# A hybrid decoder block: a pair of heads' projections between the first and second recurrent tile, w2's copies in even parts

## The chip, the cores and the metric

The kernel runs on one core of a Trainium2 chip. The metric is the device time of one execution in microseconds (us), lower is better. The core has TensorE (PE, matmuls; PEld is its weight load), VectorE (DVE), ScalarE (ACT), GpSimd (POOL) and the sync engine (SP, which here only issues transfers), and 16 DMA engines that all queues share.

## The reference, cut to what matters

```python
D_MODEL, SEQ, N_ATTN_HEADS, HEAD_DIM, LRU_WIDTH, CONV_WIDTH, D_FF = 1024, 2048, 8, 64, 512, 4, 4096
DILATED_PATTERNS = ((128, 1), (512, 4), (2048, 16))

def hybrid_mixer(h, w_in, conv_w, conv_b, w_r, b_r, w_i, b_i, lam, w_out):
    z = h @ w_in
    q, k, v, xr, gr = jnp.split(z, [512, 1024, 1536, 2048], axis=-1)
    attn = dilated_attention(q, k, v)          # 8 heads, three windows, joined by their denominators
    xr = causal_depthwise_conv(xr, conv_w, conv_b)
    rec = rg_lru(xr, w_r, b_r, w_i, b_i, lam) * jax.nn.gelu(gr)
    return jnp.concatenate([attn, rec], axis=-1) @ w_out

def rg_lru(x, w_r, b_r, w_i, b_i, lam):
    r, i = sigmoid(x @ w_r + b_r), sigmoid(x @ w_i + b_i)      # block by block
    log_a = -LRU_C * r * jax.nn.softplus(-lam)
    a, u = jnp.exp(log_a), jnp.sqrt(-jnp.expm1(2.0 * log_a)) * (i * x)
    return scan(h[t] = a[t] * h[t-1] + u[t])

def reference(x, ...):
    h = rms_norm(x, mix_norm_pre)
    x = x + rms_norm(hybrid_mixer(h, ...), mix_norm_post)
    h = rms_norm(x, mlp_norm_pre)
    a = jax.nn.relu(h @ w_ff_in)
    return x + rms_norm((a * a) @ w_ff_out, mlp_norm_post)
```

## The kernel before

The 2048 rows are worked on in two halves of 1024. Every float32 factor of a large matmul is split into a high and a low part of a faster matmul type (`split`: the high part is a copy on ACT, `L54`, the low part a subtraction, `L55`, on DVE or on POOL), and a product is three matmuls for each of 8 blocks of the inner dimension (`L198` to `L200`): 24 matmuls of 128x512 for one 128-column tile of weights and one block b of 512 rows. The product goes to one of two PSUM banks of the tag "P", and PE can start the next but one product when DVE has emptied the bank.

The input projection makes two kinds of steps. A *pair of heads* (`qkv`, written q and half and pair, as q11) has six products: q, k and v, each for two blocks. For q and k DVE scales the product (zn, `L225`, `L228`), and zn is split into zh and zl, which SP stores to DRAM in four pieces of 128 KB each; for v PE transposes zn, the two halves of vs are made on ACT and DVE, and SP stores vs. zh, zl and vs have one buffer each. The names carry the column tile: q11 has tiles 1, 5 and 9, q12 has 2, 6, 10, q13 has 3, 7, 11. A *recurrent tile* (`recurrent`, r10 to r13 in the second half) has four products, one for the conv input (tiles 12 to 15) and one for the gate (16 to 19) for each block. Behind each conv input DVE empties the bank (`L304`), keeps the last three columns for the next block (`L305`; `L303` brings them in again), runs three steps of the convolution (`L310`), and two small matmuls with their gates follow (`L313`, `L315`), then the scan (`L331`, `L332`); POOL starts the convolution (`L307`) and makes a part of the gelu (`L338` to `L340`). Weights are loaded by `load_w` one step's first tile ahead, two transfers of 256 KB each, and split. Which engine makes the low parts is `pj.lo`: POOL at first, DVE from the line `pj.lo = nc.vector` on.

The order of steps is written in three strings. `ORDER` is the first half with its attention (a0 to a3, one pair of heads each) and q10; then `BETWEEN` and `LATER`. In this stage no order of instructions is written by hand: a scheduler places the instructions of all steps on their engines, each engine runs them in that order, and so the attention a3 and the rest of a2 fill PE's gaps in the steps that follow. At its end each pair of attention is joined (`join`: its weights in jt up to `L691`, to DRAM and back as co in two parts, `L700`, and on POOL `L718`, `L721`, `L724`); the buffer co is single, so its second load waits for `L721` of the first.

Beside the steps there are three streams. `copies` are transfers from DRAM to DRAM on POOL's queue (`L1550`): w_out first, then 32 for w2, 256 and 512 KB in turns. `early_factors` makes, for the first two column pairs of the MLP's first weights, seven sums and splits each: four loads er of 256 KB, and 14 stores sf of 256 KB each on POOL's queue; it is a generator, and each `next` runs it one step on. `load_wo` loads the eight tiles woL of the output weights (512 KB each) and splits them, 16 pieces, on ACT and DVE; their memory is free when the recurrent tiles' and the attention's is. After the three strings the output projection begins (m, `L857`).

Of the kernel before, what the change touches and what calls it, by code (L numbers as in the profile page):

```python
# [37 lines left out]
def f32(ap):  # L38
    return ap.bitcast(F32)
# [12 lines left out]
def split(nc, hi, lo, src, lo_eng=None):  # L52

    return (nc.scalar.copy(out=hi, in_=src),  # L54
            (lo_eng or nc.vector).tensor_tensor(out=lo, in0=src, in1=f32(hi), op=ALU.subtract))  # L55
# [719 lines left out]
def split_there(nc, hi, lo, lo_eng=None):  # L775

    split(nc, hi, lo, f32(lo), lo_eng)
# [44 lines left out]
def mix_columns(nc, sh, scr, hf, order, t):  # L822

    mx = {}
    for g0 in range(0, KT, 4):
        n = f"{hf}_{t}_{g0}"
        hi, lo = sh.pair(f"m{n}", (P, 4, P))
        k0 = order[g0]
        sh.mixed = nc.sync.dma_start(out=f32(lo), in_=scr["mix"][hf][k0:k0 + 4, :, t * P:(t + 1) * P].rearrange("k p t -> p k t"))
        split_there(nc, hi, lo, nc.vector if hf and t == 0 else nc.gpsimd)  # L830
        for i, k in enumerate(order[g0:g0 + 4]):
            mx[k] = (hi[:, i, :], lo[:, i, :])
    return mx
# [164 lines left out]
def early_factors(nc, sh, scr, w1, j):  # L998

    v, g = nc.vector, nc.gpsimd  # L1000
    raw = [sh.s(f"er{j}_{i}", (P, KH, P)) for i in range(4)]
    a11, a12, a21, a22 = raw
    for i, t in enumerate(raw):
        nc.sync.dma_start(out=t, in_=w1[2 * j + i // 2][:, (i % 2) * KH:(i % 2 + 1) * KH])
    yield
    f = {}

    def made(m, src=None):
        if src is None:
            split_there(nc, *f[m])  # L1010
        else:
            f[m] = sh.pair(f"e{j}_{m}", (P, KH, P))
            split(nc, *f[m], src)
        for d, t in zip(scr["f"][j, m], f[m]):
            g.dma_start(out=d, in_=f32(t).rearrange("p k t -> p (k t)"))

    def sub(m, x, y, op=ALU.subtract):
        f[m] = sh.pair(f"e{j}_{m}", (P, KH, P))
        v.tensor_tensor(out=f32(f[m][1]), in0=x, in1=y, op=op)

    sub(5, a21, a22, ALU.add)
    sub(7, a11, a21)
    sub(6, f32(f[5][1]), a11)
    v.tensor_tensor(out=a21, in0=a12, in1=f32(f[6][1]), op=ALU.subtract)
    made(7)
    yield
    made(6)
    made(5)
    yield
    for m, t in ((1, a11), (2, a12), (4, a22), (3, a21)):  # L1030
        made(m, t)
        yield
# [408 lines left out]
NJ = FT // 2  # L1441
# [5 lines left out]
def trunk(tc, x, xT, g1, g2, g3, g4, w_in, conv_w, conv_b, w_r, b_r, w_i, b_i, lam, w_out, w1, w2,  # L1447
          ident_d, sel_d, mask_a, mask_b, out):
    nc = tc.nc
    out = out[0].rearrange("(b m c) d -> b c m d", m=P, c=NC)  # L1450

    def sb(name, side):
        return tc.tile_pool(name=name, bufs=1, side=side, reuse_waits="tile")
# [5 lines left out]
    with (  # L1459
# [16 lines left out]
        def halves(shape, dt, n, nm):  # L1476
            return [[d.tile(shape, dt, name=f"s{nm}{hf}_{i}") for i in range(n)] for hf in range(2)]

        scr = {
            "q": halves([2, 2, HD, HT], F32R, NP, "q"),  # L1480
            "k": halves([2, 2, HD, HT], F32R, NP, "k"),
            "v": halves([HT, 2 * P], F32R, NP, "v"),
            "co": halves([2, 2, HT], F32, NP, "co"),
            "mix": [d.tile([KT, P, HT], F32, name=f"smix{hf}") for hf in range(2)],
            "x2": [d.tile([P, D], F32, name=f"sx2{i}") for i in range(S // P)],
            "a": [[d.tile([P, 7, TB], F32, name=f"sa{hf}_{j}") for j in range(NJ)] for hf in range(2)],
            "b": [d.tile([P, 4, TB], F32, name=f"sb{j}") for j in range(NJ)],
# [10 lines left out]
        def bank(tag, name):  # L1498
            if tag in RINGS:
                turn[tag] += 1  # L1500
                tag = RINGS[tag][turn[tag] % 3 - 1]
            return banks.tile([P, TB], F32, tag=tag, bufs=BANKS[tag], name=name)
# [3 lines left out]
        def load_wo(hf, between=lambda: None):  # L1506
            return load_w_out(tc, wst.enter_context(sb(f"wo{hf}", "right")), scr["wout"], hf, order, cst, between)

        with contextlib.ExitStack() as st:
            p1a = st.enter_context(sb("p1a", "left"))  # L1510
            p1 = st.enter_context(sb("p1", "left"))
            lst = contextlib.ExitStack()
            pl = lst.enter_context(sb("lru", "left"))
            pj = Project(tc, p1, p1a, pl, bank, cst, scr, x, xT, g1, w_in)
            pj.recurrent_consts(conv_w, conv_b, w_r, b_r, w_i, b_i, lam)
            with sb("x0", "right") as px:
                w = {12: pj.load_start(12, px)}
                w[16] = pj.load_w(0, 16, nc.vector, px)
                w[13] = pj.load_w(0, 13, nc.vector, px)
                pj.load_norm(0, px)  # L1520
                w[17] = pj.load_w(0, 17, nc.gpsimd, px)
                pj.spread_norm(0)
                pj.load_x(1, px)
                pj.load_norm(1, px)
                pj.spread_norm(1)
                pj.recurrent(0, (0, 1), w, px)
                pj.load_norm(2, px)
                pj.load_norm(3, px)
            products = [(t[0], *map(int, t[1:])) for t in f"{ORDER} {BETWEEN} {LATER}".split() if t[0] in "qr"]

            copies = [(scr["wout"][k], w_out[k]) for k in order]
            for j in range(NJ):
                copies += [(scr["w2"][j][:, 0], w2[2 * j][:, 0:TB]),
                           (scr["w2"][j][:, 1:3], w2[2 * j + 1].rearrange("p (a d) -> p a d", a=2))]

            def run(steps):
                for kind, *arg in [(t[0], *map(int, t[1:])) for t in steps.split()]:
                    if kind == "q":
                        pj.qkv(*arg)
                    elif kind == "r":  # L1540
                        pj.recurrent(arg[0], (arg[1],))
                    elif kind == "a":
                        attend(*arg)
                    else:
                        pj.load_x(*arg)
                        pj.spread_norm(*arg)
                    n = 8 if kind == "r" and arg[0] else 1 if len(copies) > 2 * NJ else 0
                    with tc.issue_after(cst["pool"].ins):
                        for dst, src in copies[:n]:
                            nc.gpsimd.dma_start(out=dst, in_=src)  # L1550
                    del copies[:n]
                    if kind in "qr":
                        products.pop(0)
                        if products:
                            nxt, hf, i = products[0]
                            pj.load_ahead(hf, i if nxt == "q" else 12 + i)

            place = {"S": ("B", "B"), "pT": ("T", "T"), "o": ("O", "T")}
            with sb("at0", "right") as pa:
                attend = attention(tc, pa, lambda k, n: bank(place[k][0], n), cst, scr, 0, mask_a, mask_b, pa)  # L1560
                run(ORDER)
            pg = per.enter_context(sb("g2", "right"))
            sh = Shared(pg, bank)
            run(BETWEEN)
            lst.close()
            wo = load_wo(0)
            pj.lo = nc.vector
            early = [early_factors(nc, sh, scr, w1, j) for j in range(2)]
            for step in LATER.split():
                run(step)  # L1570
                for _ in range(5):
                    if early and next(early[0], True):
                        early.pop(0)
            for rest in early:
                for _ in rest:
                    pass
            ready = [mix_columns(nc, sh, scr, 0, order, t) for t in range(2)]
# [86 lines left out]
FIRST = 0  # L1664
SH = 2
ORDER = "q00 r02 q01 a0 r03 q02 a1 q03 x2 x3 a2 q10 a3"
BETWEEN = "r10 r11 r12 r13"
LATER = "q11 q12 q13"


def _by_residue(t):
# [51 lines left out]
```

## Time and profile before

| what | before |
|---|---|
| median of 3 runs | 2249.12 us (2246.18 to 2250.0) |
| the profiled execution | 2251.3 us, its span 2249.5 us |
| mean granted clock of PE | 0.986 |
| busy in the span: PE, DVE, ACT, POOL | 96%, 67%, 55%, 20% |
| DMA engines, mean | 210 GB/s |

The span reaches from the first to the last instruction of the profiled execution. Busy times are of the whole span; stretches with another limit are hidden in them, so the change is read from the windows and timelines of its own stretch.

### The profile page before, as it was taken

Reading aid. Unit: us, or ns where it says so; the run is one execution under the profiler, and the core shown is the slowest. Engines: PE = TensorE matmul, PEld = TensorE weight load, DVE = VectorE, ACT = ScalarE, POOL = GpSimd, SP = SyncE. Lnnn points to the kernel's source line nnn. Section 1 sums busy time; section 2 is a strip of 40 time slices with the busy share of each in tenths; the row PEclk is TensorE's granted clock in tenths of the full one; section 3 lists DMA queues with packets and bytes.
Section 4 is the critical chain, followed back from the end, with each engine's and each line's share of the span. In section 5 each row is a group of like instructions: output and inputs, shape, how many; then the busy total and the mean of one; then the engine's idle time right before and its main releaser. Section 6 shows DMA issues by size and latency. Waiting matters only on the chain.

```text
span 2249.5 us, 30781 instructions
## 1 busy us (share of the span) xinstructions
PE 2170.8 (96%) x10264; PEld 1777.6 (79%) x10264; DVE 1506.0 (67%) x2908; ACT 1233.1 (55%) x2489; POOL 453.0 (20%) x545
## 2 busy tenths in 40 slices
PE   8999989989999999999999999989999999999998
PEld 6678878767788788887888787778878888888887
DVE  6767465987748777774667677776766556646456
ACT  7646464655434555554766666754455555654442
POOL 5543414455223001011001111113200000000003
PEclk9999999999999999999999999999999999999999
DMA  8365674555975677869777777777553444776665
GB/s 285 101 185 177 181 240 146 181 156 165 336 248 169 227 266 279 301 257 299 219 212 225 209 233 216 219 224 227 182 185 129 170 140 164 272 237 191 194 196 179
DMA packets 223360, 473.51 MB, mean 210 GB/s; under 512 B 23536, under 2 KB 77712, under 8 KB 216928
## 3 DMA queue, kind: packets, MB, share of 16 engines
q1 hardware_dynamic: 193856, 336.34, 47.6%
q0 software_dynamic: 29344, 135.20, 17.2%
q8 instruction: 81, 1.33, 0.2%
q14 instruction: 79, 0.65, 0.1%
HBM read 337.09 MB, written 151.13 MB: 217 GB/s over the span
## 4 chain that ended last, share of the span: by engine, by line
PE 74%; DVE 9%; DMA 6%; ACT 3%; issue 3%; SPq 1%; POOL 1%; DVEq 0%; ACTq 0%; POOLq 0%
PE o L1222 8%; PE o L1221 8%; PE o L1223 8%; PE za L1072 5%; PE za L1073 5%; PE za L1071 5%; PE z L198 3%; PE z L199 3%; PE z L200 3%; PE m L859 3%; PE m L857 3%; PE m L858 3%; PE zc L1073 2%; PE zc L1072 2%; PE zc L1071 2%
## 5 line engine op out<-in xcount | busy, mean ns | idle before, releaser
L198 PE MATMUL z<-hH,wH 128*128 128x512 f32 x640 | 262.3, 410 | 19.0 <-ACT wH L54 7.4
L199 PE MATMUL z<-hL,wH 128*128 128x512 f32 x640 | 259.6, 406 | 0.6 <-DVE hL L173 0.6
L200 PE MATMUL z<-hH,wL 128*128 128x512 f32 x640 | 258.5, 405 | 0.5 <-DVE wL L55 0.5
L198 PEld LDWEIGHTS z<-hH,wH 128*128 128x128 f32 x640 | 122.1, 191 | 55.3 <-DVE xr L304 9.9
L199 PEld LDWEIGHTS z<-hL,wH 128*128 128x128 f32 x640 | 122.0, 191 | 31.2 <-issue 4.3
L200 PEld LDWEIGHTS z<-hH,wL 128*128 128x128 f32 x640 | 122.3, 191 | 30.1 <-issue 4.4
L420 ACT ACTIVATE smB<-smB,stB 128x128 f32<-128x128 f32 (+3 forms) x128 | 71.6, 560 | 89.5 <-DVE stB L414 89.3
L1076 ACT ACTIVATE sq<-sq 128x512 f32<-128x512 f32 x93 | 58.8, 632 | 85.8 <-DVE sq L1080 85.8
L55 POOL TENSOR_TENSOR wL<-wraw,wH 128x512 fp32r<-128x512 f32 x58 | 82.3, 1435 | 78.6 <-ACT wH L54 75.9
L55 DVE TENSOR_TENSOR tlB<-pT_B,thB 128x384 fp32r<-128x384 f32 x96 | 57.0, 598 | 50.0 <-ACT thB L54 46.2
L1136 POOL DMA_DIRECT2D sa<-sq x31 | 16.5, 532 | 363.7 <-ACT sq L1077 353.1
L54 ACT CAST wH<-wraw 128x512 fp32r<-128x512 f32 (+1 forms) x81 | 47.2, 612 | 66.2 <-DMA wraw<-in_dram 33.5
L420 ACT ACTIVATE sm<-sm,stA 128x256 f32<-128x256 f32 (+1 forms) x128 | 63.1, 495 | 27.3 <-DVE stA L414 26.9
L1077 ACT ACTIVATE sq<-sq 128x512 f32<-128x512 f32 x124 | 76.1, 628 | 1.9
L1255 POOL TENSOR_TENSOR y<-y,g4b 128x512 f32<-128x512 f32 x8 | 12.4, 1580 | 259.3 <-ACT junk_y L84 259.3
L414 DVE CUSTOM_DVE_ANT_0 smB<-SB,mask_b 128x128 f32<-128x128 f32 (+3 forms) x128 | 59.3, 482 | 6.8 <-PE pT_B L393 5.2
L55 DVE TENSOR_TENSOR tlA<-pT,thA 128x512 fp32r<-128x512 f32 (+1 forms) x64 | 42.3, 669 | 26.0 <-ACT thA L54 25.6
L54 ACT CAST thB<-pT_B 128x384 fp32r<-128x384 f32 x96 | 48.4, 509 | 17.3 <-PE pT_B L393 9.6
L640 PE MATMUL oB<-thB,vb 128*128 128x256 f32 x192 | 48.4, 282 | 9.8 <-ACT thB L54 9.0
L393 PE MATMUL pT_B<-ident,smB 128*128 128x128 f32 x320 | 53.0, 283 | 1.1 <-DVE na L409 0.9
L414 DVE CUSTOM_DVE_ANT_0 sm<-S,mask_a 128x256 f32<-128x256 f32 (+1 forms) x128 | 47.5, 410 | 8.7 <-PE pT L393 4.0
L1071 PE MATMUL zc<-hHT,f_7H 128*128 128x512 f32 x128 | 50.7, 396 | 1.9 <-ACT hHT L54 1.9
(607 smaller groups left out, 7053.3 us busy)
## 6 DMA issues: line engine op xcount, KB each, us to landing
sa<-as POOLq DMA_DIRECT2D x31, 1024.0 KB, 6.5
w1r<-in_dram SPq DMA_DIRECT2D x56, 512.0 KB, 4.0
sa<-sq POOLq DMA_DIRECT2D x31, 768.0 KB, 3.9
wraw<-in_dram SPq DMA_DIRECT2D x79, 256.0 KB, 3.9
place<-in_dram SPq DMA_DIRECT2D x14, 1024.0 KB, 7.6
sb<-place POOLq DMA_DIRECT2D x14, 1024.0 KB, 5.2
kh<-sk SPq DMA_DIRECT2D x24, 512.0 KB, 4.9
kl<-sk SPq DMA_DIRECT2D x24, 512.0 KB, 7.6
```

The costliest lines, as they stand in the source:

```text
L55: (lo_eng or nc.vector).tensor_tensor(out=lo, in0=src, in1=f32(hi), op=ALU.subtract))
L198: pe.matmul(z, hi[:, k, :], hh, start=(k == 0), stop=False)
L199: pe.matmul(z, hi[:, k, :], hl, start=False, stop=False)
L200: pe.matmul(z, lo[:, k, :], hh, start=False, stop=(k == KT - 1))
L414: v.tensor_tensor_reduce(out=sm[:, c0:c0 + w], in0=sp[:, c0:c0 + w], in1=mask[:, mask.shape[-1] - w:], scale=1.0, scalar=3.0e38, op0=ALU.a ...
L420: s.activation(out=sm[:, c0:c0 + w], in_=sm[:, c0:c0 + w], func=AF.Exp, scale=-1.0, bias=st[:, 0, u, cols[j]:cols[j] + 1], accum_out=st[:, ...
L1071: pe.matmul(o, hi[:, k], bh[:, k], start=start and k == 0, stop=False, skip_group_check=True)
L1072: pe.matmul(o, hi[:, k], bl[:, k], start=False, stop=False, skip_group_check=True)
L1073: pe.matmul(o, lo[:, k], bh[:, k], start=False, stop=k == KH - 1, skip_group_check=True)
L1221: pe.matmul(o, ah[:, ts], bh, start=fresh and j == 0, stop=False, skip_group_check=True)
L1222: pe.matmul(o, ah[:, ts], bl, start=False, stop=False, skip_group_check=True)
L1223: pe.matmul(o, al[:, ts], bh, start=False, stop=j == NJ - 1, skip_group_check=True)
```

## The change

q11 moves from `LATER` to the place between r10 and r11. `early_factors` is set up before `BETWEEN`; its steps run five after q11, six after q12 and six after q13, where they ran five after each. Since `pj.lo` is switched after `BETWEEN`, q11's low parts are now POOL's. The 32 copies of w2 go out in parts of six behind each of q10, r10, q11, r11, r12 and two behind r13, where it was eight behind each recurrent tile.

```diff
-                    n = 8 if kind == "r" and arg[0] else 1 if len(copies) > 2 * NJ else 0
+                    n = 1 if len(copies) > 2 * NJ else 6 if kind in "qr" and arg[0] else 0
                     with tc.issue_after(cst["pool"].ins):
                         for dst, src in copies[:n]:
                             nc.gpsimd.dma_start(out=dst, in_=src)
...
-            run(BETWEEN)
+            early = [early_factors(nc, sh, scr, w1, j) for j in range(2)]
+
+            def some(n):
+                for _ in range(n):
+                    if early and next(early[0], True):
+                        early.pop(0)
+
+            for step in BETWEEN.split():
+                run(step)
+                some(5 if step == "q11" else 0)
             lst.close()
             wo = load_wo(0)
             pj.lo = nc.vector
-            early = [early_factors(nc, sh, scr, w1, j) for j in range(2)]
             for step in LATER.split():
                 run(step)
-                for _ in range(5):
-                    if early and next(early[0], True):
-                        early.pop(0)
+                some(6)
...
-BETWEEN = "r10 r11 r12 r13"
-LATER = "q11 q12 q13"
+BETWEEN = "r10 q11 r11 r12 r13"
+LATER = "q12 q13"
```

What the scheduler makes of it, at three places. First PE, at the end of r10's products (z_16_1 is r10's last product; S and SB are scores, pT and oB transposes and values of the attention). Before:

```order
L200 MATMUL z_16_1_4690<-hH_7_3336,wL_16_4540 128x512
L198 MATMUL z_13_0_4753<-hH_0_3231,wH_13_4733 128x512
L199 MATMUL z_13_0_4753<-hL_0_3232,wH_13_4733 128x512
L200 MATMUL z_13_0_4753<-hH_0_3231,wL_13_4734 128x512
L557 MATMUL S_6_0_4090<-kh_6_4080,qa_6_4083 128x128
```

and after:

```order
L200 MATMUL z_16_1_4696<-hH_7_3336,wL_16_4546 128x512
L198 MATMUL z_1_0_4747<-hH_0_3231,wH_1_4737 128x512
L199 MATMUL z_1_0_4747<-hL_0_3232,wH_1_4737 128x512
L313 MATMUL pr_0_1_4677<-xc_0_1_4672,bd_r 128x512
L393 MATMUL pT_0_5_0_0_3595<-ident,sm_5_0_3584 128x128 x3
```

The attention of heads 5 and 6 now stands among q11's products (z_1, z_5, z_9), where it stood among those of r11 (z_13, z_17) and r12; the last of it stands in r13's second block, where it stood in q11.

Second, at the join of pair 2 (co_2). On SP, before, the join's loads stand among loads of weights for r12 and r13:

```order
L693 DMA sco_2_97<-jt_2_3791 16x128 x2
L110 DMA wraw_18_1_4953<-in_dram 128x512
L700 DMA co_2_0_3806<-sco_2_97 64x512 x4
L110 DMA wraw_15_0_5143<-in_dram 128x512
L110 DMA wraw_15_1_5147<-in_dram 128x512
L700 DMA co_2_1_3815<-sco_2_97 64x512 x4
L110 DMA wraw_19_0_5153<-in_dram 128x512
```

and after, with the stores of q11's k (sk_1) and v (sv_1) round them:

```order
L693 DMA sco_2_97<-jt_2_3791 16x128 x2
L110 DMA wraw_17_0_5039<-in_dram 128x512
L700 DMA co_2_0_3806<-sco_2_97 64x512 x4
L236 DMA sk_1_84<-zl_5_1_4890 64x512 x2
L110 DMA wraw_17_1_5043<-in_dram 128x512
L700 DMA co_2_1_3815<-sco_2_97 64x512 x4
L244 DMA sv_1_92<-vs_9_0_4939 128x4x256
```

DVE's rows behind that join, after:

```order
L228 TENSOR_TENSOR zn_9_1_4968<-z_9_1_4943,bc_3353 128x512
L55 TENSOR_TENSOR vs_9_0_4939<-vt_9_0_4934,vs_9_0_4939 128x8x64
...
L55 TENSOR_TENSOR vs_9_1_4975<-vt_9_1_4970,vs_9_1_4975 128x8x64
L304 TENSOR_TENSOR xr_1_0_5072<-z_13_0_5047,bc_3290 128x4x128
L305 COPY tail<-xr_1_0_5072 128x3
```

The join moved from beside r12 to beside q11's v, and r11's first `L304` now follows the second vs directly.

Third, in q12 and q13, where the output weights are loaded and split. On SP the loads of the first er stood behind all woL; after, they stand ahead of them:

```order
L1004 DMA er_3_4998<-in_dram 128x512
L236 DMA sq_2_77<-zl_2_1_5762 64x512 x2
L110 DMA wraw_3_0_5933<-in_dram 128x512
L110 DMA wraw_3_1_5937<-in_dram 128x512
L235 DMA sk_2_85<-zh_6_0_5806 64x512 x2
L236 DMA sk_2_85<-zl_6_0_5807 64x512 x2
L792 DMA woL_4_5658<-swo_205 128x1024
```

On DVE the splits of woL stood between zn_9_1 and zn_6_0, that is in q11's end and q12's begin. After, they stand in q12's end and q13's begin:

```order
L55 TENSOR_TENSOR woL_4_5658<-woL_4_5658,woH_4_5657 128x512
L55 TENSOR_TENSOR woL_5_5656<-woL_5_5656,woH_5_5655 128x512 x2
L55 TENSOR_TENSOR woL_6_5654<-woL_6_5654,woH_6_5653 128x512 x2
L55 TENSOR_TENSOR woL_7_5652<-woL_7_5652,woH_7_5651 128x512 x2
L228 TENSOR_TENSOR zn_10_1_5920<-z_10_1_5895,bc_3353 128x512
L55 TENSOR_TENSOR woL_0_5650<-woL_0_5650,woH_0_5649 128x512 x2
...
L55 TENSOR_TENSOR woL_2_5646<-woL_2_5646,woH_2_5645 128x512 x2
L225 SCALAR_TENSOR_TENSOR zn_3_0_6008<-z_3_0_5983,bc_3290 128x512
L55 TENSOR_TENSOR woL_3_5644<-woL_3_5644,woH_3_5643 128x512 x2
```

The output weights moved some two steps later on both engines, past the first er and its sums.

## Rows read from the trace of the kernel before

**Rows 1.** The page: the chain that ended last, by engine.

```profile
PE 74%; DVE 9%; DMA 6%; ACT 3%; issue 3%; SPq 1%; POOL 1%; DVEq 0%; ACTq 0%; POOLq 0%
```

**Rows 2.** Windows: us, busy time and count by engine, granted clock, DMA share, GB/s.

```profile
374.00:540.00 166.00, 151.24 (x768) 118.18 (x767) 143.29 (x265) 103.70 (x210) 83.35 (x91) 0.97 0.50 154
540.00:636.00 96.00, 92.48 (x408) 74.24 (x407) 58.08 (x94) 35.98 (x64) 30.50 (x43) 1.00 0.87 289
```

**Rows 3.** Waits of PE, 374 to 540 us: total, times, longest.

```profile
PE z L198 <- DVE xr L304: 7.2, 4, 5.4
PE pr L313 <- DVE state L332: 2.2, 1, 2.2
```

**Rows 4.** Windows of 10 us, columns as in rows 2.

```profile
460.00:470.00 10.00, 6.63 (x24) 4.02 (x22) 10.00 (x8) 1.49 (x3) 9.14 (x8) 0.88 0.24 79
470.00:480.00 10.00, 5.68 (x17) 4.52 (x18) 9.75 (x10) 4.40 (x6) 7.26 (x10) 0.60 0.42 122
```

**Rows 5.** Timeline of DVE: start us, us, line, operation.

```profile
465.43 1.68 DVE L310 SCALAR_TENSOR_TENSOR xc<-xr,cw,xc 128x512 f32<-128x512 f32 x1
...
467.15 6.16 DVE L303 COPY xr<-tail 128x3 f32<-128x3 f32 x1
```

**Rows 6.** Timeline of POOL in the same stretch.

```profile
464.51 2.05 POOL L718 TENSOR_TENSOR na<-na,co 128x512 f32<-128x512 f32 x1
...
470.80 2.48 POOL L55 TENSOR_TENSOR wL<-wraw,wH 128x512 fp32r<-128x512 f32 x2
```

**Rows 7.** Groups of DVE by line, 374 to 540 us: count, busy us, mean ns.

```profile
L310 DVE SCALAR_TENSOR_TENSOR xc<-xr,cw,xc 128x512 f32<-128x512 f32 x24 | 24.5, 1019 | 0.2
...
L304 DVE TENSOR_TENSOR xr<-z,bc 128x512 f32<-128x512 f32 x8 | 8.6, 1073 | 0.0
...
L332 DVE COPY state<-xc 128x1 f32<-128x1 f32 x8 | 1.2, 146 | 0.0
...
L55 DVE TENSOR_TENSOR vs<-vt,vs 128x512 fp32r<-128x512 f32 x1 | 0.7, 668 | 0.0
```

**Rows 8.** Windows of 20 us, columns as in rows 2.

```profile
540.00:560.00 20.00, 20.00 (x89) 16.27 (x88) 12.94 (x22) 5.10 (x9) 9.09 (x9) 1.00 0.53 160
560.00:580.00 20.00, 19.91 (x91) 16.14 (x90) 13.42 (x22) 10.96 (x20) 3.33 (x4) 1.00 0.91 303
580.00:600.00 20.00, 18.35 (x82) 14.35 (x81) 13.44 (x22) 8.68 (x16) 7.49 (x14) 1.00 1.01 361
600.00:620.00 20.00, 18.23 (x81) 14.45 (x80) 14.82 (x24) 7.76 (x14) 7.49 (x14) 1.00 1.00 330
```

**Rows 9.** Groups of POOL by line, 374 to 540 us.

```profile
L55 POOL TENSOR_TENSOR wL<-wraw,wH 128x512 fp32r<-128x512 f32 x14 | 20.3, 1471 | 12.5 <-ACT wH L54 12.3
L1550 POOL DMA_DIRECT2D sw<-in_dram x32 | 16.8, 532 | 0.0
```

**Rows 10.** Timeline of all engines: the join of pair 2.

```profile
439.26 0.27 DVE L691 TENSOR_TENSOR jt<-jt 16x128 f32<-16x128 f32 x1
...
457.34 1.29 POOL L721 TENSOR_TENSOR nb<-nb,co 128x512 f32<-128x512 f32 x1 [1.14 <-DMA co<-sco]
...
458.65 1.73 SPq L700 DMA_DIRECT2D co<-sco  x3
```

**Rows 11.** DMA issues, 370 to 660 us: count, KB each, median us to landing.

```profile
woL<-swo SPq DMA_DIRECT2D x8, 512.0 KB, 6.4
sv<-vs SPq DMA_DIRECT2D x7, 512.0 KB, 4.5
...
er<-in_dram SPq DMA_DIRECT2D x8, 256.0 KB, 7.4
...
sf<-e_7H POOLq DMA_DIRECT2D x2, 256.0 KB, 3.3
```

**Rows 12.** Timeline, SP's and POOL's queue, 560 to 590 us.

```profile
562.17 11.19 SPq L792 DMA_DIRECT2D woL<-swo  x8
...
585.58 0.54 POOL L1015 DMA_DIRECT2D sf<-e_7H  x1 [21.07 <-ACT e_7H L54]
```

## Prediction

> **What bounds the kernel now.** The table above has TensorE (PE) busy for 96% of the span, and the page gives it 74% of the chain that ended last [rows 1], so a change pays only where PE waits. The change moves work between the end of the first half's attention and the output projection, so I cut that stretch in two with the view of windows [rows 2]. From 374 us (the first recurrent tile, r10, is under way) to 540 us (the last attention matmuls are just done) PE is busy 151.2 of 166 us and waits **14.8 us**, at a mean granted clock of 0.97; VectorE (DVE) is busy 143.3 us, nearly as much as PE. From 540 to 636 us, where the output projection begins, PE waits only 3.5 us, but the DMA engines are busy 0.87 of the time. So before 540 us DVE is the second limit, and after it DMA is.
>
> What ended PE's waits before 540 us: the largest group is a projection's first matmul that waits for DVE's `L304`, which empties the bank that the matmul wants, 7.2 us in four waits, and the next a gate's matmul behind `L332`, 2.2 us, together **9.4 us** [rows 3]. Two windows of 10 us hold most of it: PE busy 6.6 and 5.7 us there, at a clock of 0.88 and 0.60 [rows 4]. The timelines show the cause: DVE's `L303`, a copy of 128x3 numbers, stands for 6.16 us [rows 5] while POOL runs one instruction after the other, and ends just as POOL's two `L55` end, at 473.3 us [rows 6]. `L304` comes next on DVE, and PE's longest wait for it is 5.4 us [rows 3]. Just ahead `L310` takes 1.68 us, against a mean of 1.02 [rows 5, 7]. What POOL does there is the join of attention pair 2 (`L718` to `L724`) together with the recurrent tile's gate and weights.
>
> **The change, part by part.** (1) *q11 between r10 and r11.* Its matmuls are the same and only stand earlier (first order piece). Until attention ends PE now runs r10, q11, r11, r12 and half of r13, where it ran all four recurrent tiles and a third of q11. The recurrent lines of DVE, 13 groups from `L310` (24.5 us) to `L332` (1.2 us), sum to 105.1 us in the stretch, which is 13.1 us for each of 8 half tiles [rows 7]. A half tile less saves 13.1 us of DVE; of q11 the old stretch had 2 zn and 4 splits, 6 instructions at about the 0.67 us of vs [rows 7], 4 us, and a whole q11 without its splits costs 6 zn and 2 vs, 5.4 us. DVE: 143.3 - 13.1 - 4 + 5.4 = 132 us. PE: two of q11's products were in the stretch and four more come, two recurrent products leave, at 24 matmuls of 0.22 us each (91 in 19.9 us [rows 8]) about 10 us more, so 161 us. DVE's load falls from 0.95 of PE's to 0.82. It doesn't fall everywhere: with r11, r12 and the half of r13 it stays near one.
>
> What of the 14.8 us goes? Nothing, if DVE's stalls only move; all, if the lower load suffices. I take the 9.4 us of [rows 3], which gather round the join. In DVE's new order (second piece) the join stands beside the v part of q11, whose DVE rows read PSUM (zn, vs) and hold no copy, and the next copy of a tail comes behind the `L304` that PE wants. The other 5.4 us stay. **-9.4 us** (0 to -14.8).
>
> The Trainium skill, SBUF — State Buffer, "Who interferes with whom", says that a copy of this kind and a POOL instruction lock the same port, and that the second blocks until the first ends. By one POOL instruction the copy would wait at most 2.05 us, the longest one there [rows 6]; the trace shows 6.16 us, across several of them, so I go by the row. By the rule alone the term would be some 4 us smaller.
>
> (2) *Clock.* In the two windows PE was busy 6.63 us at 0.88 and 5.68 us at 0.60 [rows 4]; at full clock that work would be 0.8 and 2.3 us shorter. The deep one followed the long wait; if that goes, so does it: **-2.3 us** (0 to -3.1).
>
> (3) *The splits of q11* go from DVE to POOL, since `pj.lo` is still POOL there: six weight halves and four zl at 1.47 us [rows 9], 14.7 us more on POOL, less half a recurrent tile's share. POOL is busy 83 of 166 us [rows 2], so it has room: 0. If it hadn't, it would show in the next term.
>
> (4) *A new chain at the join.* The v store of q11 now stands on SP behind the join's second load `co_2_1` (second piece). That load waits for POOL's `L721`; the buffer `vs` is single, so the second vs waits for the store, and DVE's `L304` of r11 stands right behind it; PE's z_13_1 needs the bank that this `L304` empties. From the end of the join's weights (`L691`, 439.5 us) to the issue of the second load, 458.7 us, it took 19.1 us [rows 10]. Add 1.7 us of issue, 4.5 us for a landing of sv [rows 11], 1.3 for the two halves of vs and 1.1 for `L304` [rows 7]: 28 us. PE has about 125 matmuls between zn_5_1 and z_13_1, 27.5 us at 0.22. So it is even; six copies of w2 (6 x 0.53 us on POOL [rows 9] and 2.25 MB) stand right ahead of the join and can add up to 8 us. **+2 us** (0 to +8).
>
> (5) *The end of the stage* gets shorter for DMA. From the end of attention to the output projection PE has 349 rows where it had 393, about 10 us less: 82 of the former 92.5 us. What has to move in it stays, all but q11's stores: 289 GB/s over 96 us [rows 2] is 27.7 MB, less some 2.7 MB is 25 MB; among it 4 MB of output weights, 2 MB of er and 7 MB of sf stores (28 of 256 KB) [rows 11]. The first 20 us have little to move, 160 GB/s, 3.2 MB. So 21.8 MB fall on 62 us, and the next three windows carried 303, 361 and 330 GB/s [rows 8]: 66 us at their mean of 331. **+4 us** (0 at 361 GB/s, +10 at 303). What is late: in the third piece er now stands ahead of the output weights on SP and the splits of the weights, each behind its load, between DVE's zn_6_1 and zn_3_0, zn_3_1; these empty the banks that z_3_1 and z_7_0 want. PE's old waits there stay.
>
> (6) *w2 evenly.* 32 copies in DRAM at 0.53 us of POOL [rows 9], 6 for each step and not 8: nothing new on POOL's time as a whole. The first six come behind q10, 3.2 us ahead of a split of r10's weights on POOL; 0, since the weights are loaded one product ahead, and 3.2 us if that cover is gone. The last come with r13, as before.
>
> Sum on the profiled execution (2251.3 us): -9.4 - 2.3 + 2 + 4 = -5.7, so 2245.6 us. The median of the runs shown lies 2.2 us lower (2249.1): **2243.4 us**, 0.25% faster. What a measurement here can tell from no change is 0.2%, 4.5 us.
>
> **The rivals.** *A: the stalls only move.* r11 to half of r13 carry 5 of 8 half tiles, and POOL's burst meets r11's copies. Speaks for it: DVE's load there stays near one. Against it: half of the attention is past by then. Gain 3 us, no clock back, +2, +4: 2252 us, no measurable change.
>
> *B: the end is not DMA-bound.* The sf stores are wanted by nobody before the MLP and er can start as soon as attention's memory is free. Terms 1 to 3 stand, term 5 is 0: 2239.4 us.
>
> *C: slower, by the output weights.* At the 303 GB/s of their window [rows 8] their 4 MB take 13 us. Now er and the first 3.5 MB of sf are in flight with them: 4 + 3.5 + 2 MB at 331 GB/s is 28.7 us, 16 us later for the last splits, with zn_10_1, zn_3_0 and zn_3_1 queued between them on DVE and PE waiting for these. If nothing covers it, term 5 is 16 and not 4: 2255.4 us, 0.3% slower. PE's two banks cover some 10 us of it; it decides from 14 us on, or from less if term 1 falls short too. The Trainium skill, DMA: Bandwidth & Descriptors, "Issuing engines are not separate DMA queues", says that POOL's and SP's transfers run on the same 16 engines and interleave; by it the sf stores do take half of the weights' rate. In the trace of before they were hardly in flight together: the weights' issue ended at 573.4 us, 6.4 us ahead of their landing [rows 11], and the first sf came at 585.6 us [rows 12], so no run here shows it.
>
> **How the numbers follow.** The forecast 0.45, A 0.22, B 0.13, C 0.20. The forecast's own spread (2239 to 2248) leaves 0.09 within 0.2%, and of A and C about 0.02 and 0.20 are slower. Faster 0.36 + 0.13 = 0.49; same 0.09 + 0.20 = 0.29; slower 0.22. The bounds of the terms together reach from 2231 to 2267; leaving out one in ten at either end the range is 2234 to 2256 us. For the forecast's own sign it would be 2234 to 2245.
>
> **What would show it.** Right: no DVE copy over 2 us beside r11 and r12, no window at a clock under 0.9 before attention ends, under 8 us of PE's waits up to there. Term 4: a wait of z_13_1 for `L304`, with `L55` of vs ahead of it waiting for the store of v. Term 5: waits of z_3_1, z_7_0 or z_11_0 for zn, wH or wL, with the DMA engines full. I am wrong if PE's waits with r11 and r12 stay at 9 us or more, or if the end of the stage costs over 10 us.

## The result, and the profile after

| | before | after |
|---|---|---|
| median | 2249.11 us (14 runs) | 2258.61 us (14 runs, 2250.89 to 2263.31) |
| ratio, with its 95% interval | | **1.0038** (1.0027 to 1.0048) |
| profiled execution, its span | 2251.3, 2249.5 us | 2255.0, 2253.2 us |

The change makes the kernel 9.5 us slower and the prediction is wrong: the forecast was 2243.4 us, the range ended at 2256. The windows of the changed kernel that answer to [rows 2] and [rows 4] (columns as there), the last three where the granted clock fell:

```profile
374.00:540.00 166.00, 157.15 (x821) 125.47 (x820) 120.33 (x246) 93.53 (x199) 84.30 (x84) 1.00 0.49 157
540.00:636.00 96.00, 82.86 (x331) 63.73 (x330) 72.75 (x102) 42.95 (x71) 40.08 (x50) 0.93 0.76 260
550.00:560.00 10.00, 7.65 (x26) 5.18 (x25) 9.89 (x9) 2.95 (x4) 7.95 (x7) 0.85 0.56 172
560.00:570.00 10.00, 6.40 (x19) 4.08 (x18) 8.48 (x11) 7.13 (x9) 5.24 (x4) 0.81 0.54 170
610.00:620.00 10.00, 6.03 (x17) 4.79 (x18) 9.23 (x17) 6.88 (x13) 4.25 (x8) 0.66 0.98 328
```

Up to 540 us PE now waits 8.85 us and not 14.76, and at full clock. From 540 to 636 us it waits 13.1 us and not 3.5, at 0.93. The waits of PE from 374 to 700 us (us in total, times, longest), which answer to [rows 3]:

```profile
PE z L198 <- ACT wH L54: 5.3, 1, 5.3
PE pi L315 <- ACT r L318: 4.3, 2, 3.6
PE pr L313 <- DVE xc L310: 3.4, 3, 2.3
PE oB L640 <- DVE nb L409: 2.4, 2, 1.8
PE pT L393 <- DVE tlB L55: 2.3, 2, 1.3
PE z L198 <- DVE zn L228: 1.8, 1, 1.8
PE z L200 <- POOL wL L55: 1.4, 1, 1.4
...
PE z L198 <- DVE xr L304: 0.3, 1, 0.3
```

`L304` has gone from 7.2 to 0.3 us; new at the top are `wH`, `pi` and `pr`. The timelines place them. One place is r13's second half, of PE first, then of DVE:

```profile
556.71 1.83 PE L313 MATMUL pr<-xc,bd_r 128*128 128x512 f32 x2 [2.35 <-DVE xc L310]
564.18 2.08 PE L315 MATMUL pi<-xc,bd_i 128*128 128x512 f32 x2 [3.60 <-ACT r L318]
```

```profile
550.83 1.78 DVE L326 TENSOR_TENSOR a<-r 128x512 f32<-128x512 f32 x1
552.53 2.76 DVE L310 SCALAR_TENSOR_TENSOR xc<-xr,cw,xc 128x512 f32<-128x512 f32 x1
...
557.27 1.58 DVE L330 TENSOR_TENSOR i<-i,th 128x512 f32<-128x512 f32 x1
558.77 1.09 DVE L55 TENSOR_TENSOR wL<-wraw,wH 128x512 fp32r<-128x512 f32 x1
559.78 2.29 DVE L331 TENSOR_TENSOR_SCAN xc<-r,state,i 128x512 f32<-128x512 f32 x1
```

DVE is busy 9.9 of 10 us there. The other place is q13's second weight; SP's queue, then PE:

```profile
585.65 7.85 SPq L792 DMA_DIRECT2D woL<-swo  x8
593.60 2.29 SPq L235 DMA_DIRECT2D sk<-zh  x2
597.51 2.69 SPq L1004 DMA_DIRECT2D er<-in_dram  x2
602.21 2.77 SPq L236 DMA_DIRECT2D sk<-zl  x2
606.88 2.24 SPq L1004 DMA_DIRECT2D er<-in_dram  x2
609.16 0.91 SPq L110 DMA_DIRECT2D wraw<-in_dram  x2
```

```profile
613.97 0.80 PE L198 MATMUL z<-hH,wH 128*128 128x512 f32 x1 [5.28 <-ACT wH L54]
```

The weight (`wraw`) is issued at 609.2 us, behind eight loads of woL and four of er, at each of which SP waits for a woL to land:

```profile
SPq L1004 <- DMA woL<-swo: 6.9, 4, 1.9
```

woL itself is issued at 585.7 us, where it was 562.2 [rows 12], and takes this to land (KB each, median us), where it took 6.4 [rows 11]:

```profile
woL<-swo SPq DMA_DIRECT2D x8, 512.0 KB, 12.5
```

One row sums it up, the last product of the first half's output projection on PE, whose group of 64 matmuls ends at 722.9 us before and after at

```profile
L857 PE MATMUL m<-woH,m_0H x64: 389/389/497, 639.8 to 729.9; 128*128 128x512 f32 x64
```

7.0 us later. From there on the two run nearly alike (1527 and 1523 us to the end of the span).

**One measure for all kernels.** From windows of 10 us I add PE's idle time, and (1 - granted clock) x PE's busy time as the clock's loss; busy time alone, since an idle PE has nothing to lose by its clock. In all 20 kernels the end of that group less both sums (370 to 700 us) is 697 to 703 us, and with the sums of 0 to 370 us taken off too it is 671 to 674 us, so these sums tell nearly all of the differences. The sums from 0 to 370 us, ahead of the moved steps, run from 24.9 to 30.9 us (before 28.6, after 29.2), so a few us of one execution say little.

| kernel (edits below) | ratio (95% interval) | 370-540: idle + clock | 540-700: idle + clock | group ends |
|---|---|---|---|---|
| before | 1 | 14.8 + 3.1 | 3.5 + 0 | 722.9 |
| after | 1.0038 (1.0027-1.0048) | 8.8 + 0 | 14.3 + 4.4 | 729.9 |
| b_w2 | 1.0054 (1.0036-1.0072) | 17.3 + 7.4 | 6.1 + 3.7 | 737.0 |
| b_early | 1.0037 (1.0025-1.0049) | 15.7 + 3.0 | 12.2 + 4.7 | 733.7 |
| q_only | 1.0080 (1.0055-1.0105) | 10.4 + 1.9 | 20.2 + 7.9 | 742.2 |
| b_w2early | 1.0069 (1.0043-1.0094) | 15.4 + 6.5 | 11.6 + 3.9 | 739.7 |
| a_oldw2 | 1.0054 (1.0030-1.0078) | 10.5 + 1.4 | 18.9 + 7.9 | 739.5 |
| a_late | 1.0098 (1.0085-1.0111) | 7.5 + 2.9 | 23.6 + 7.4 | 743.4 |
| q10_btw | 1.0061 (1.0045-1.0077) | 11.4 + 6.0 | 12.1 + 3.2 | 736.0 |
| a_er1 | 1.0044 (1.0028-1.0059) | 8.5 + 1.4 | 14.8 + 7.7 | 733.1 |
| a_er1x | 1.0099 (1.0084-1.0114) | 7.8 + 2.7 | 30.3 + 6.5 | 746.3 |
| a_join | 1.0034 (1.0023-1.0045) | 8.8 + 1.6 | 12.7 + 5.2 | 731.0 |
| a_er1xlo | 1.0069 (1.0054-1.0084) | 6.8 + 0 | 24.4 + 7.0 | 738.6 |
| a_r2 | 1.0025 (1.0011-1.0040) | 7.1 + 0 | 14.1 + 4.9 | 729.4 |
| a_half | 1.0012 (0.9997-1.0026) | 8.3 + 1.3 | 11.7 + 3.6 | 723.5 |
| a_er1s | 1.0085 (1.0060-1.0109) | 6.8 + 4.4 | 24.3 + 6.7 | 741.8 |
| a_er1sr2 | 1.0070 (1.0045-1.0095) | 7.5 + 4.2 | 22.8 + 3.4 | 737.5 |
| b_join | 0.9997 (0.9981-1.0013) | 13.4 + 3.2 | 2.7 + 1.7 | 719.7 |
| b_tail | 1.0003 (0.9991-1.0015) | 10.7 + 5.9 | 5.0 + 1.2 | 723.6 |
| b_tailj | 0.9988 (0.9979-0.9997) | 12.2 + 3.3 | 3.4 + 1.6 | 717.5 |

### The profile page after: what moved, and what is told of

The parts are those of the page before. It is cut to its first block, busy times and chain, and to the rows that moved or that the text cites. A ratio compares the mean times of both kernels' runs of the same rounds, so it can differ in the third digit from the quotient of the medians.

```text
span 2253.2 us, 30786 instructions
## 1 busy us (share of the span) xinstructions
PE 2172.2 (96%) x10264; PEld 1777.0 (79%) x10264; DVE 1495.6 (66%) x2898; ACT 1231.9 (55%) x2489; POOL 468.5 (21%) x555
## 4 chain that ended last, share of the span: by engine, by line
PE 61%; DVE 7%; DMA 7%; ACT 4%; issue 2%; POOL 1%; SPq 1%; DVEq 0%; ACTq 0%; POOLq 0%
PE o L1221 8%; PE o L1222 8%; PE o L1223 8%; PE za L1072 5%; PE za L1073 5%; PE za L1071 5%; PE m L859 3%; PE m L858 3%; PE m L857 3%; PE zc L1072 2%; PE zc L1073 2%; PE zc L1071 2%; PE oB L640 1%; PE zb L1073 1%; PE zb L1072 1%
## 5 line engine op out<-in xcount | busy, mean ns | idle before, releaser
L198 PE MATMUL z<-hH,wH 128*128 128x512 f32 x640 | 263.9, 413 | 15.2 <-ACT wH L54 10.5
L55 POOL TENSOR_TENSOR wL<-wraw,wH 128x512 fp32r<-128x512 f32 x64 | 90.9, 1437 | 78.8 <-ACT wH L54 50.9
L55 DVE TENSOR_TENSOR tlA<-pT,thA 128x512 fp32r<-128x512 f32 (+1 forms) x64 | 42.6, 670 | 29.5 <-ACT thA L54 29.2
L1072 PE MATMUL za<-hLT,f_5H 128*128 128x512 f32 x128 | 50.7, 396 | 2.1 <-DVE hLT L55 2.1
```

Of the source, the lines that this page charges most:

```text
L198: pe.matmul(z, hi[:, k, :], hh, start=(k == 0), stop=False)
L1072: pe.matmul(o, hi[:, k], bl[:, k], start=False, stop=False, skip_group_check=True)
```

## The experiments

Ratios are to the kernel before on the same chip. Labels with b edit the kernel before, with a the changed one; q_only and q10_btw edit the kernel before too.

**1. The parts of the change alone and in pairs.** b_w2 takes the line of `n`, b_early the lines of `early_factors` (five steps ahead of `load_wo`, six after q11 and q12 each), q_only the two strings. b_w2early, a_oldw2 and a_late are the pairs: without q11's move, without w2, without the early factors.

> The kernel before with w2's copies spread evenly, and nothing else of the change. Theory 'weights behind the output weights' (the loss lies at 600 to 615 us of the changed kernel, where PE waits 5.3 us for wH of q13's second weight, whose load stands on SP behind eight loads of woL that wait for r13's end, and behind four loads of er1) and theory 'early factors' (their earlier splits and stores cost): no difference, 2247 to 2251 us. Theory 'w2': the spread copies take DMA share in the stage with attention and cost 4 us or more: 2253 us or above.

> The kernel before, with q11 in its old place after r13, but the early factors set up ahead of the output weights, as in the changed kernel; w2 as before. Theory 'weights behind': r13 is long done when woL's loads are issued, so they go about 3 us later than before (er0's 1 MB ahead of them) and the end of the stage costs at most 3 us: 2248 to 2252 us, and no wait of PE for wH over 3 us at 600 to 630 us. Theory 'early factors': most of the 9.5 us comes here, 2255 us or above.

> The kernel before with q11 between r10 and r11, and nothing else of the change. Theory 'the output weights wait for r13': q11 puts r13's end later, and with the old w2 transfers woL's eight loads stand on SP even behind the last weight of q13; m_0 waits for them, so the first product of the output projection waits over 5 us and the time is 2258 us or more. Rival 'the move is good, its two companions are bad' (w2 even alone gave +11.7 us and the early factors alone +8.6 us): 2240 to 2247 us, faster than before.

> The kernel before with both companions and q11 in its old place. If the costs of the two add (11.7 and 8.6 us), 2265 to 2270 us; if both meet the same limit at the end of the stage (the same 20 MB have to pass in some 60 us), 2255 to 2260 us. With the changed kernel (all three) at 2258.6 us, the first case says that the move itself is worth 8 to 10 us when the companions are there, the second that it is worth nothing.

> The changed kernel with w2's transfers as before. Theory 'the output weights wait for r13': woL again stands behind q13's last weight, 2256 us or more, slower than or like the changed kernel. Rival 'companions are bad' (w2 even costs 11.7 us by itself): 2246 to 2249 us, about 10 us below the changed kernel.

> The changed kernel with q11 between r10 and r11 and w2 even, but the early factors set up after the output weights, as before. Theory 'weights behind': woL still waits for r13's end and is issued after 575 us; er1 now stands behind the second weight of q13, so PE's wait for that weight falls from 5.3 to 3 us or less, and the time is 2252 to 2257 us. Theory 'early factors': the loss is gone, 2243 to 2249 us.

Every part alone makes the kernel slower: w2's transfers by 0.54%, the early factors by 0.37%, the move by 0.80%. So b_w2's expectation of no difference falls, and with q_only the rival "the companions are bad". The parts do not add. The early factors with the move cost 0.54% and not 1.17% (a_oldw2), w2 with the move 0.98% and not 1.34% (a_late, slower than both of its theories); for w2 with the early factors, 0.69% against 0.91%, the interval leaves it open. All three together cost 0.38%. With both companions there the kernel is no slower with the move than without it (0.38% against 0.69%, intervals that just overlap).

What q_only shows is the place of the output weights: in the row of SP its woL starts at

```profile
625.39 9.49 SPq L792 DMA_DIRECT2D woL<-swo  x8
```

and PE's sums after 540 us rise to 20.2 + 7.9 us. Not all of that is woL's: 9.1 us of the idle time stand at 540 to 570 us, 7.7 of them one gate's wait for `L332`, and m_0 waits 2.1 us where over 5 were expected. In the twelve kernels with q11 between r10 and r11, woL is first issued at 581.7 to 625.4 us, in the eight others at 553.5 to 577.1, and in none before r13 is done on DVE: in a_er1xlo its last row (`L343`) ends at 581.45 us and woL starts at 581.72. (In before r13's last store stands at 549 us, in after at 582.7.) What holds woL shows in SP's waits within the eight loads. In before it is attention's last store, in a_er1xlo r13's:

```profile
SPq L792 <- DMA smix<-na: 7.0, 1, 7.0
```

```profile
SPq L792 <- DMA smix<-ge: 3.1, 1, 3.1
```

All eight kernels of the old place wait so for attention, 3.1 to 7.0 us. In after no such wait stands: SP comes to woL only behind q12's stores, where the scheduler has put it. That it is put there for its memory (that of the recurrent tiles, whose pool is closed just ahead of `load_wo`, and of attention) is read from the code; no run here moves it to other memory. Where the early factors stand matters both ways: ahead of woL they cost 0.37% without the move (a wait of 7.8 us for vs up to 590 us), and behind woL 0.60% more with it (a_late against after; a wait of 7.4 us for vs up to 642 us). What b_w2 loses before 540 us (24.7 us against 17.9) was not taken apart: with it the scheduler orders PE's instructions anew from the first projection on.

**2. q10 instead of q11 between r10 and r11** (ORDER then ends in "a2 a3"), so that r13 ends no later.

> The kernel before in which q10, not q11, is moved between r10 and r11 (from ahead of the last attention pair); r13 then ends as early as before, early factors and w2 as before. Theory 'the output weights wait for r13': woL is issued near 562 us as before, the waits for r11's copies (7.2 us) go, no wait comes at the end of the stage: 2238 to 2247 us. Rival 'any shift loses' (the order of before is a local optimum, each shift makes a wait of 5 us or more and the clock falls with it): 2252 to 2262 us.

r13 did end early (`L345` at 545 us), yet woL went at 577.1 us, since attention ended later (its last store is issued at 577.4 us and not 563.9, and SP waits 3.1 us for it), and the last wait is one of 8.2 us for vs up to 642 us. The rival holds.

**3. The weight behind woL and er1: order or bytes?** a_er1: `some(3)` for `some(6)`. a_er1x and a_er1s queue the loads of er1 on SP behind q13's last weight (`wload` below), and behind q13's last store with `ready`, the mix's columns, ahead of them:

```diff
-                some(6)
+                some(1)
+            with tc.issue_after(cst["wload"].ins):
+                next(early[-1])
```

a_half stores half of each early factor and later reads that half twice, so it leaves a part of the result out:

```diff
-            g.dma_start(out=d, in_=f32(t).rearrange("p k t -> p (k t)"))
+            g.dma_start(out=d[:, 0:TB // 2], in_=f32(t).rearrange("p k t -> p (k t)")[:, 0:TB // 2])
```

> The changed kernel, in which only three steps instead of six of the early factors follow q12 and q13 each, so that er1's four loads stand behind q13's second weight on SP. Theory 'weights behind': that weight comes earlier by the 1 MB that stood ahead of it, at the 420 GB/s that its stretch moved 2.5 us: PE's wait for it 5.3 to about 2.8 us, the time 2255 to 2257 us. Rival 'transfers are full anyway': what is taken from ahead of the weight returns as a wait for the next load, the time stays at 2258 to 2260 us.

> The changed kernel with er1's four loads queued on SP behind the last weight of q13 and nothing else altered on PE. Theory 'two places' (of the changed kernel's loss about half lies at 550 to 570 us, where the join of pair 3 on POOL meets r13 on DVE: 6 us of waits and 3 us of clock; the other half at 600 to 615 us, where q13's second weight stands behind woL and er1: 7 us of waits and 3 us of clock): the waits at 600 to 615 us fall from 7.1 to 4 us or less, the waits at 550 to 570 us stay at 6 us; 2252 to 2256 us, if nothing behind waits for er1's factors. Rival 'the bytes are the limit, not their order' : the wait moves to the next weight or to m_0, 2257 us or more.

> The changed kernel with only half of each early factor stored to DRAM (3.7 of 7.3 MB less at 580 to 640 us; later the stored half is read twice, so part of the result is left out). Theory 'bytes' (the transfers of the end of the stage, 0.97 to 1.04 of all DMA queues, set the wait for q13's second weight): the waits at 600 to 615 us fall from 7 to 3 us or less, 2248 to 2254 us. Rival 'order' (the weight stands behind woL on SP, whatever the stores do): the wait stays at 5 us, 2256 to 2260 us.

> The changed kernel with er1's loads, and so its factors and their stores, behind the last store of q13 on SP, and the columns of the mix loaded ahead of them. Theory 'bytes': 1 MB of loads and 3.7 MB of stores leave the stretch of 595 to 640 us, which is full, for 650 to 690 us, where queues are 0.5 busy: the waits at 600 to 615 us fall from 7 to 4 us or less, no wait for m_0H over 2 us, 2248 to 2254 us. Rival 'moved, not removed' (as with er1 behind the last weight, where m_0H came 15.6 us late): a wait of 5 us or more at 640 to 730 us, 2256 us or more.

PE's waits of a_half from 590 to 660 us:

```profile
PE z L198 <- DVE zn L228: 1.6, 1, 1.6
PE vt L240 <- DVE zn L228: 1.6, 1, 1.6
PE z L198 <- ACT wH L54: 1.1, 1, 1.1
PE z L198 <- DVE zn L225: 1.1, 1, 1.1
```

In a_half the weight stands on SP behind the same eight loads of woL and four of er. With 3.7 MB of stores less, 1.8 of them ahead of this weight, it is issued at 605.0 us and not 609.2; PE's wait for wH, which begins at 608.7 us in both, falls from 5.3 to 1.1 us; no window after 570 us has a clock under 0.9; idle and clock from 570 to 700 us fall from 10.4 to 5.4 us, and the ratio from 1.0038 to 1.0012, with intervals that do not overlap. So the bytes bear on it, and not the order alone. Two things in this execution are not theirs: woL itself begins 2.0 us earlier, as the first stores go out, and of the 6.4 us by which the group ends earlier, 4.0 lie ahead of 370 us. The waits from 600 to 620 us are 3.8 us, a little over the 3 that were expected.

The three other edits move the same bytes: the wait for wH falls as expected (2.2, 3.3 and 2.4 us), and a longer one comes behind it. In a_er1 it is one of 2.9 us for a vs, and the ratio stays (1.0044). In a_er1x PE waits for the output projection's left side:

```profile
PE m L857 <- ACT m_0H L54: 15.6, 1, 15.6
```

since ACT stands 15.62 us at a vs whose single buffer waits for its store, which SP issues only at 643.6 us, behind k's stores and g3b. In a_er1s it is 12.9 us, for a later column, whose load stands on SP behind g2b, and g2b waits 7.1 us for DVE's `e_1L`. The rival "moved, not removed" holds for both.

**4. r13's second half.** a_join: `e = v if hf or pr == 3 else g`, the join of pair 3 on DVE. a_r2: r of r13's second half from another pool's buffer. a_er1xlo is a_er1x with the low halves on DVE from r12 on, a_er1sr2 is a_er1s with a_r2.

> The changed kernel in which the join of pair 3 multiplies and adds on DVE, not on POOL (6 instructions, at 0.68 us 4.1 us more for DVE, and 6 by 1.3 to 2.0 us less for POOL). Theory 'two places, the first by POOL beside DVE': DVE's L310 and scan instructions at 550 to 570 us return to 0.7 and 1.7 us, the waits there fall from 6 to 3 us or less and the clock with them, 2252 to 2256 us. Rival 'DVE is simply full there' (5.0 of 5 us at 550 to 555): the waits stay at 6 us or grow, 2257 to 2263 us.

> The changed kernel in which the gate r of r13's second half has a buffer of its own. Theory 'r's only buffer' (at 562 us ACT's r waits 4 us for DVE's scan of the first half, which still reads r; PE's pi waits 3.6 us for ACT's r; with the join on DVE instead of POOL this wait was the same, 4.2 us): the wait of pi for r falls under 1 us, the clock's 3 us at 550 to 570 us shrink, 2250 to 2255 us. Rival 'DVE is full there': another wait for DVE (pr for xc, z for zn) takes its place, 2256 us or more.

> As the kernel with er1 behind q13's last weight, and DVE instead of POOL makes the low halves from r12 on. On SP woL then stands right behind q13's first weight. Theory 'two places': both losses shrink, 2244 to 2252 us. Rival 'DVE is full at 550 to 570 us': six more splits there (4.1 us) lengthen the waits of 6 us to 9 or more, 2257 us or more.

> Both of the last two edits on the changed kernel: r of r13's second half in its own buffer, er1 behind q13's last store. If both places are as the theories say, their gains add: 2241 to 2249 us, at or below the kernel before. If one of them fails, as that one alone.

a_join does free DVE's instructions: the `L310` of 2.76 us takes 1.09, the scan 1.28 for 2.29. But six more instructions stand on DVE, and PE's two waits are 2.1 and 4.2 us, as long as before (2.3 and 3.6): my theory that they fall with the join does not hold. In a_r2 pi no longer waits 3.6 us for r; a wait of 2.9 us for zn takes its place. From 540 to 640 us:

```profile
PE z L198 <- ACT wH L54: 5.6, 1, 5.6
PE z L198 <- DVE zn L225: 2.9, 1, 2.9
PE pr L313 <- DVE xc L310: 2.4, 1, 2.4
```

So r's buffer was only the last to be released: DVE is busy 9.9 of 10 us in both windows from 550 to 570 us. How much of that is DVE's own work and how much instructions held beside POOL, as the `L310` of 2.76 us, no run here separates, since a_join takes the one away and adds to the other. In a_er1xlo, with more splits on DVE, pi waits 8.1 us, but DVE is busy only 7.7 and 8.2 of 10 us there: ACT's r stands behind `L341`, which waits 3.1 us for POOL's `L340`. The ratios of a_join and a_r2 (1.0034, 1.0025) cannot be told from that of after. a_er1sr2 lies between its two parts and misses their sum (2263.2 us, not 2241 to 2249).

**5. The burst of before at the join of pair 2, without moving q11.** b_join: `e = v if hf or pr == 2 else g`. b_tail puts the two copies of 128x3 on ACT for the second half (`(s.copy if hf else v.tensor_copy)(...)`). b_tailj is both.

> The kernel before in which the join of pair 2, beside r11, multiplies and adds on DVE, not on POOL. Theory 'POOL beside DVE' (term 1 of the prediction): the copy of 6.16 us falls under 2 us, the waits of 9.4 us at 465 to 475 us fall to 5 us or less, and the clock's 5 us with them: 2238 to 2246 us. Rival 'DVE is full' (0.95 busy there): 4.1 us more on DVE cost as much as the freed port gives, 2247 us or more.

> The kernel before with the two copies of 128x3 (L303, L305) of the second half's recurrent tiles on ACT instead of DVE. Theory 'the copy itself' (beside POOL's burst one copy took 6.16 us and PE then waited 5.45 us for xr; with the join of pair 2 on DVE the longest copy took 0.58 us): no operation of DVE takes over 3 us at 455 to 480 us, PE's waits there fall from 7.7 to 4 us or less, 2240 to 2246 us. Rival 'DVE's load beside POOL': the time that the copy took falls on the next DVE instruction, waits and time stay, 2247 to 2252 us.

> The kernel before with the copies on ACT and the join of pair 2 on DVE. If the two take away different delays, PE's waits at 440 to 480 us fall under 5 us (7.7 before, 8.0 with the join on DVE alone) and the time is 2236 to 2243 us, below the kernel before; if DVE's load alone decides, 2242 to 2248 us.

In b_join the longest `L303` takes 0.58 us (6.16 before, [rows 5]), but DVE now stands 5.1 us at the join's first product until its factors land, and PE waits 5.6 us for the `L310` behind it; ratio 0.9997. In b_tail the delay falls on the next of DVE's instructions beside POOL's join:

```profile
462.34 4.40 DVE L330 TENSOR_TENSOR i<-i,th 128x512 f32<-128x512 f32 x1
```

```profile
462.44 1.29 POOL L721 TENSOR_TENSOR nb<-nb,co 128x512 f32<-128x512 f32 x1
463.68 1.27 POOL L340 TENSOR_TENSOR ge<-ge,gr 128x512 f32<-128x512 f32 x1
464.91 1.27 POOL L724 TENSOR_TENSOR na<-na,nb 128x512 f32<-128x512 f32 x1
```

The copy was not special; the rival holds (1.0003). b_tailj is the one kernel whose interval lies below the one before: 0.9988 (0.9979 to 0.9997), median 2244.86 against 2246.89 us. It keeps q11 where it was. PE's waits at 440 to 480 us are 7.1 us, not under 5, so the first case of its expectation falls. Its execution shows 15.5 us of idle and clock at 370 to 540 us, 17.9 before; its early end at 717.5 us also has 3.0 us from ahead of 370 us, where nothing was changed, so the interval carries the verdict and not this execution, and among 18 edits one interval this close to 1 is weak evidence.

## Why the prediction was wrong

*Terms 1 and 2* hold within their ranges. Idle time and clock up to 540 us fall from 14.8 + 3.1 to 8.8 + 0 us, -5.9 and -3.1 where -9.4 and -2.3 were forecast. The 9.4 us of waits that term 1 named fall to 0.3 (`L304`), but new ones, for oB, pT, pi and wL, take some 3 us back. No copy on DVE takes over 1.26 us, and no window up to 550 us is under 0.9. DVE's load against PE's fell to 0.77 (120.3 of 157.2 us; 0.82 was worked out).

*Term 3* (0) shows as a wait of 1.4 us for POOL's `wL`. *Term 4* (+2): the chain is there, ACT stands 5.1 us for the store of v ahead of the second vs, but PE was covered; z_13_1's wait for `L304` is 0.3 us.

***Term 5* is the step that failed**, "+4 us (0 to +10)". From 540 to 700 us the sums rise from 3.5 to 18.7 us, +15.2. About half of the 18.7, 7.1 us of waits (for zn and wH) and 2.1 of clock at 600 to 620 us, is what the term named: z_3_1, z_7_0 wait for zn and wH with the DMA engines full, and a_half shows that the bytes bear on it. It was mis-sized because it spread the bytes over the whole stretch: in every run woL comes behind r13, which q11 puts later, so its 4 MB (issued from 585.7 us) share the queues with 3.5 MB of sf (584.8 to 598.1 us), which came behind it before, and the weight stands behind them and er; nor did the term have a price for the clock. The Trainium skill, DMA: Bandwidth & Descriptors, "Issuing engines are not separate DMA queues", says that transfers started by different engines interleave on the same 16 DMA engines, and agrees with the row: with POOL's sf stores in flight woL took 12.5 us to land and not 6.4. Not all of the 6.1 us can be sf's: in before SP paused 7.0 us among the eight loads, and in a_half, with half of sf's bytes, they took 13.5 us.

The other half, 6.0 us of waits and 2.4 of clock at 550 to 570 us, had no term. The text noted that DVE's load with r13 "stays near one" and gave it no price; before, r13's halves ran among attention's matmuls, now only q12 is left beside them. That is rival A's "the stalls only move", to r13. Whether POOL's part in it is small stays open: a_join does not shorten the waits, but it also gives DVE six instructions more.

*Term 6* (w2, 0) is wrong alone, +0.54%; in the changed kernel the intervals tell no effect of w2's spreading (1.0038 with it, 1.0054 without it in a_oldw2). Of the rivals C came nearest, in time (2255.4) and by the output weights, though the longest wait is for q13's weight and not behind a split of woL.

Of the measured 9.5 us the profiled pair shows 7.0 at the end of the group and 3.7 at the end of the span; that execution was one of the faster ones of the changed kernel. What stays open: the 6.8 us that b_w2 loses before 540 us, what of r13's waits is DVE's work and what POOL's beside it, and whether other memory for woL would save the move.

## What to carry to other kernels

When a step moves, ask first what the step that it delays has in its memory, and which transfers may wait for that memory: their bytes then meet those behind them. Where PE has no slack, price each new wait with the clock that falls with it, here some two to three tenths of the wait (4.4 us on 14.3 in after, 6.5 on 30.3 in a_er1x). Where a scheduler orders the whole program, parts of a change do not add, so run them alone before crediting one.

## What the runs showed that was not expected

A DVE instruction beside POOL can be held over several of POOL's: the copy of before for 6.16 us, in b_tail a `L330` of two inputs for 4.40 us across three of POOL's instructions of 1.27 to 1.29 us, where it took 0.68 us in a_join. The Trainium skill, SBUF — State Buffer, "Who interferes with whom", has it that such an instruction contends with POOL's reads, which agrees, and that the second blocks until the first ends, which by itself would hold it for one of them, 1.3 us.

PE's clock fell to its lower level, 1.2 of 2.4 GHz, for all of the window from 640 to 650 us of a_er1x, in which PE did nothing, and stayed there to the end of the wait and on:

```profile
640.00:650.00 10.00, 0.00 (x0) 0.00 (x0) 0.69 (x1) 0.00 (x0) 0.00 (x0) 0.50 0.86 282
650.00:660.00 10.00, 5.66 (x13) 4.02 (x14) 0.69 (x1) 3.06 (x5) 4.63 (x4) 0.51 0.96 281
```
